# Seven-product units: the low part of unsummed weights by a negated copy and an adding transfer

## The chip, the cores and the metric

The kernel runs on one core of one Trainium2 chip. The metric is the device time of one execution in microseconds. Times of a run are medians over timed executions; a profile is one further execution with the hardware profiler on. Engine names in the profile: PE is TensorE (PEld its weight loads), DVE is VectorE, ACT is ScalarE, POOL is GpSimd, SP is SyncE, which issues the plain loads.

## What is computed

A two-layer transformer-like network with 256 latent and 256 context tokens of width 1024, in float32. Each layer is a half feed-forward, a mixer (attention in layer 0, an mLSTM in layer 1), and another half feed-forward, each modulated and normalized:

```python
def half_ffn(h, shift, scale, gate, w_in, w_out, g, b):
    xm = modulate(h, shift, scale)
    a, u = jnp.split(xm @ w_in, 2, axis=-1)
    y = (jax.nn.silu(a) * u) @ w_out
    return post_norm(h, 0.5 * gate * y, g, b)
```

`w_in` is 1024 x 5632 and `w_out` 2816 x 1024. There are four such feed-forwards; the first three run over all 512 tokens, the last over the 256 latent ones. The change touches the second half of `xm @ w_in` in the second and the third of them.

## The kernel before

Every float32 matrix product is made as three products in the faster type float32r: an operand `x` is split into a high part `h` (its rounded copy) and a low part `l = x - h`, and `mm3` adds `wh xh + wh xl + wl xh` in PSUM. A weight tile `[128, 1024]` is loaded by SP into one of three buffers of the tag `raw`. `split` then makes the parts: ScalarE casts (`h`, line 225 of before), VectorE subtracts (`l`, line 230). Both parts share one buffer of the tag `w`, of which there are 7.

The hidden columns of a feed-forward are 22 blocks `j` of 128 gate and 128 up columns, made in two halves of 11. In the second half of feed-forwards 2 and 3 (`fast` in `ffn`), `fast_in` makes a block by a scheme with seven products in place of eight: the weights are cut into `a11, a21` (buffer `r0`) and `a12, a22` (`r1`), the activations into latent and context tokens and lower and upper input rows. VectorE forms the weight sums `s1, s2, s4, s3` by four additions (line 641). Then four pairs are split: `a11` alone (512 wide), `r1`, which is `a12` and `a22` (1024 wide), `s1` with `s2`, and `s4` with `s3`. The seven products, in TensorE's order, are a11, a12, s1, s2, a22, s4, s3; each is 4 x 3 = 12 matmuls with 256 columns. ScalarE copies partial sums out after the first, third, fourth and fifth (lines 666, 669, 671, 673), applies silu (676) after the sixth, and VectorE finishes with 675, 679, 680 and the split of the result.

A scheduler in the tile framework orders each engine's instructions from its own costs; instructions that are pinned keep the program's order. Buffers of a tag are handed out as they come free. The norms use small buffers of the tag `s1` (`S1B` of them). [...]

Of the kernel before, what the change touches and what calls it, by code (L numbers as in the profile page):

```python
# [9 lines left out]
F32 = mybir.dt.float32  # L10
# [17 lines left out]
NFH = 11  # L28
# [5 lines left out]
SH = 16  # L34
# [24 lines left out]
HELD = 2  # L59
OUTAT = {18: (0,), 19: (1,), 21: (2,), 23: (3,), 25: (4,), 26: (5,)}  # L60
AHEAD = 3
S1B = 5

SQPE = ()
SQA = (7,)
# [21 lines left out]


SUMSAT = 4
FLIP = 56  # L90
BESIDE = {1: (), 2: (2, 3)}
PIECES = 4
# [50 lines left out]
class Stream:  # L143


    def __init__(self, b, chunks, sh=0):
        self.b, self.chunks, self.kept = b, chunks, (None, None)
        self.sh = sh if callable(sh) else lambda c: sh

    def __call__(self, i, w=P):  # L150
        c, o = divmod(i * P, 1024)
        if self.kept[0] != c:
            self.kept = (c, self.b.chunk(self.chunks[c], self.sh(c)))
        h, l = self.kept[1]
        return h[:, o : o + w], l[:, o : o + w]


class Keep(Stream):


    def __init__(self, b, chunks, sh=0, seen=None):
        super().__init__(b, chunks, sh)
        self.all = dict([seen.kept]) if seen else {}

    def __call__(self, i, w=P):
        c, o = divmod(i * P, 1024)
        if c not in self.all:
            self.all[c] = self.b.chunk(self.chunks[c], self.sh(c))
        h, l = self.all[c]
        return h[:, o : o + w], l[:, o : o + w]  # L170


class Body:
# [41 lines left out]
        w = self.t([P, 2 * 1024 + BLOCK], dt, tag="w", bufs=WB)  # L215
        return [w[:, i * 1024 + sh : i * 1024 + sh + n] for i in range(2)]

    def chunk(self, src, sh=0):
        r = self.raw(src)
        h, l = self.pair(sh=sh)  # L220
        self.split(r, h, l)
        return h, l

    def split(self, x, h, l):
        self.behind(self.nc.scalar.copy(h, x))  # L225
# [400 lines left out]
    def fast_in(self, j, w_in, st):  # L626

        nc, V, S = self.nc, self.nc.vector, self.nc.scalar
        half = 4 * P
        t4 = self.made[2]  # L630
        if j == NFH:
            w = self.t([P, 2 * 1024 + BLOCK], F32R, tag="w", bufs=WB)
            t4 = [w[:, FLIP + i * 1024 : FLIP + (i + 1) * 1024].rearrange("p (k f) -> p k f", f=TL) for i in range(2)]
            for i in range(2):
                S.copy(t4[i], self.made[2][i].bitcast(F32))
        r0, r1 = (self.raw(w_in[2 * j + i]) for i in range(2))
        sums = self.t([P, 4 * half], tag="sums", bufs=1, pool=st)
        part = lambda x, i: x[:, i * half : (i + 1) * half]
        a11, a21, a12, a22 = part(r0, 0), part(r0, 1), part(r1, 0), part(r1, 1)
        s1, s2, s4, s3 = (part(sums, i) for i in range(4))  # L640
        add = lambda o, x, y: V.tensor_tensor(out=o, in0=x, in1=y, op=ALU.add)  # L641
        ws = [self.pair(sh=SH, n=half)] + [self.pair(sh=SH) for _ in range(3)]
        self.split(a11, *ws[0])
        self.split(r1, *ws[1])
        add(s1, a21, a22)
        add(s2, s1, a11)
        add(s4, s2, a12)
        add(s3, a11, a21)
        self.split(sums[:, : 2 * half], *ws[2])
        self.split(sums[:, 2 * half :], *ws[3])  # L650
        w = {n: [part(x, i) for x in ws[p]] for n, p, i in (
            ("a11", 0, 0), ("a12", 1, 0), ("a22", 1, 1), ("s1", 2, 0), ("s2", 2, 1), ("s4", 3, 0), ("s3", 3, 1),
        )}
        of = lambda k0, g: lambda k: self.x(k0 + k, g)
        made = lambda i: lambda k: [x[:, k, :] for x in self.made[i]]

        def product(o, name, x, first, last):
            for k in range(ND // 2):
                c = slice(k * P, (k + 1) * P)
                self.mm3(o, [y[:, c] for y in w[name]], x(k), first and k == 0, last and k == ND // 2 - 1, group=False)  # L660

        x, yv, z = self.mm()[:, :TL], self.mm(), self.mm()[:, :TL]
        y, v = yv[:, :TL], yv[:, TL:]
        a, u = self.tmp(), self.tmp()
        product(x, "a11", of(0, LAT), True, False)
        S.copy(a[:, :TL], x)
        product(y, "a12", of(ND // 2, LAT), True, True)
        product(v, "s1", of(0, CTX), True, False)
        S.copy(u[:, TL:], v)
        product(x, "s2", made(0), False, False)  # L670
        S.copy(a[:, TL:], x)
        product(z, "a22", lambda k: [x[:, k, :] for x in t4], True, True)
        S.copy(u[:, :TL], z)
        product(v, "s4", of(ND // 2, CTX), False, True)
        V.tensor_tensor(out=a, in0=a, in1=yv, op=ALU.add)
        S.activation(a, a, AF.Silu)
        product(x, "s3", made(1), False, True)
        u2 = u.rearrange("p (n f) -> p n f", n=2)
        V.scalar_tensor_tensor(u2, x[:, None, :].broadcast_to([P, 2, TL]), -1.0, u2, ALU.mult, ALU.subtract)
        V.tensor_tensor(out=a, in0=a, in1=u, op=ALU.mult)  # L680
        gh, gl = self.gt[j] = tuple(self.t([P, self.gw], F32R, tag=k, bufs=self.gn, pool=self.gp) for k in ("gh", "gl"))
        self.split(a, gh, gl)

    def ffn(self, layer, s, gate, groups, side, start=None, cpool=None):
# [4 lines left out]
        with self.tc.tile_pool(name=f"ffn{li}", bufs=1) as gp:  # L689
# [34 lines left out]
            for hf in range(2):  # L724
                js = list(range(hf * NFH, (hf + 1) * NFH))[0 if hf else done :]
                if hf == 0 and not start:
                    first = js[:LEAD]
                    ws = {j: Keep(self, [w_in[2 * j + i] for i in range(2)], SH) for j in first}
                    assert len(self.running) == 1

                    k0, k1 = range(ND // 2), range(ND // 2, ND)
                    for j in first[:-1]:
                        unit_in(j, ws[j], LAT, LEADSTEP[li])
                    j = first[-1]
                    ps = unit_in(j, ws[j], LAT, ks=k0)
                    assert not self.running
                    xs = {}
                    for k in BESIDE[li]:
                        xs[k] = [self.t([P, self.gw], F32R, tag=t, bufs=self.gn, pool=gp)[:, FLIP : FLIP + TL] for t in ("gh", "gl")]
                        for o, x in zip(xs[k], self.x(k, CTX)):  # L740
                            nc.scalar.copy(o, x.bitcast(F32))
                    pc = unit_in(first[0], ws[first[0]], CTX, ks=k0, xs=xs)
                    ws[j](ND)
                    unit_in(first[0], ws[first[0]], CTX, ks=k1, ps=pc)
                    unit_in(j, ws[j], LAT, ks=k1, ps=ps)
                    for j in first[1:]:
                        unit_in(j, ws[j], CTX)
                    for j in first:
                        call("in", j)
                    js = js[LEAD:]  # L750
                fast = cpool is not None and hf == 1
                for j in js:
                    if fast:
                        self.fast_in(j, w_in, st)
                        continue
                    unit_in(j, stream(j), allg)
                    assert not self.running
                    if j >= LEAD + FAFTER:
                        self.fine = False
                    call("in", j)  # L760
                    self.residual(2, self.pin)
                if not hf:
                    self.residual(len(self.later))
                w = Stream(self, [w_out[hf * NFH + i] for i in range(NFH)])
                body = ND - TAIL if hf else ND
                if fast:
                    more.close()
                    cpool = self.silu_all()
                for d in range(body):
                    if cpool and not hf and d == SUMSAT:  # L770
                        self.flush()
                        cpool.close()
                        self.n += 1
                        more = ExitStack()
                        st = more.enter_context(self.tc.tile_pool(name=f"st{self.n}", bufs=1, side="right"))
                        self.fast_operands(st)
                    unit_out(hf, d, w, allg)
                    if cpool and not hf and d >= SUMSAT and d - SUMSAT < 2:
                        self.fast_sums(d - SUMSAT)
                    call("out", hf, d)  # L780
                if body < ND:
                    w = Keep(self, w.chunks, SH, w)
                    self.fine = True
                    for g in groups:
                        for d in range(body, ND):
                            unit_out(hf, d, w, g, TAILSTEP)
                    self.steps('B')
# [981 lines left out]
```

## Time and profile before

| | us |
|---|---|
| median of 3 runs | 1626.13 (1625.94 to 1628.58) |
| span of the profiled execution | 1625.5 |
| TensorE busy | 1606.9 (99%) |
| VectorE busy | 1355.7 (83%) |
| ScalarE busy | 749.2 (46%) |
| GpSimd busy | 63.0 (4%) |

The profiled execution is listed by its span, from the first to the last instruction; 1625.5 us is 0.6 us under the median of the timed runs. The first of the two stretches with seven-product units lies from about 742 to 847 us of the span, the second from about 1094 to 1199 us. A busy share is an average over stages; which engine ends a stage is read from the waits within it.

### The profile page before, as it was taken

The page shows a single profiled execution, that of the slowest core. Times are in us where ns is not written, and L with a number is a line of the kernel's source. Part 1 is how long each engine was busy: PE and PEld are TensorE (multiplying, and loading weights), DVE is VectorE, ACT ScalarE, POOL GpSimd, SP SyncE. Part 2 cuts the span into 40 slices and gives each one's busy share as a digit, 9 for nine tenths or more (in the row PEclk, how much of TensorE's full clock was granted, in tenths as well). Part 3 has the DMA queues.
Part 4 walks back from the last instruction along what each step waited for, and adds up shares of the span by engine and source line. Part 5 has one row for each costly group of instructions (what it writes and reads, how often), then busy time and mean ns, then how long its engine had stood idle before and what let it go on. Part 6 is the DMA issues. An engine that isn't in the chain of part 4 may idle for free. (4 is left out here: it accounts for less than half of the span.)

```text
span 1625.5 us, 26587 instructions
## 1 busy us (share of the span) xinstructions
PE 1606.9 (99%) x10304; PEld 1451.7 (89%) x10304; DVE 1355.7 (83%) x2699; ACT 749.2 (46%) x1272; POOL 63.0 (4%) x77
## 2 busy tenths in 40 slices
PE   9999999999999999999999999999999999999998
PEld 7888888889988998889998998889999989999987
DVE  7899977649889879899986879699966968897687
ACT  6522132314676443316652444336652657566542
POOL 0000000001011100000000100000001000030000
PEclk9999999999999999999999999999999999999999
DMA  9687766422202447633445258713363343437552
GB/s 358 221 252 237 235 205 187 137 66 85 66 1 80 151 134 221 219 117 105 129 146 180 79 165 289 253 58 118 104 225 100 98 130 87 142 110 253 181 176 91
DMA packets 72222, 251.56 MB, mean 155 GB/s; under 512 B 7960, under 2 KB 10776, under 8 KB 72096
## 3 DMA queue, kind: packets, MB, share of 16 engines
q1 hardware_dynamic: 71520, 249.09, 47.7%
q8 instruction: 80, 1.31, 0.3%
q10 hardware_dynamic: 576, 0.79, 0.1%
q14 instruction: 46, 0.38, 0.1%
HBM read 248.79 MB, written 1.05 MB: 154 GB/s over the span
## 5 line engine op out<-in xcount | busy, mean ns | idle before, releaser
L241 PE MATMUL t<-t,t 128*128 128x256 f32 (+2 forms) x8412 | 1317.0, 318 | 6.4 <-ACT t L225 3.3
L241 PEld LDWEIGHTS t<-t,t 128*128 128x128 f32 x8412 | 1185.7, 188 | 125.4 <-ACT t L225 4.7
L225 ACT CAST t<-t 128x1024 fp32r<-128x1024 f32 (+3 forms) x521 | 428.5, 844 | 485.8 <-PE t L241 214.5
L230 DVE TENSOR_TENSOR t<-t,t 128x256 fp32r<-128x256 f32 (+2 forms) x740 | 513.8, 729 | 111.9 <-ACT t L225 107.7
L350 DVE SCALAR_TENSOR_TENSOR t<-t,t 128x1024 bf16<-128x1024 f32 x224 | 260.7, 1220 | 0.0
L588 ACT ACTIVATE t<-t 128x512 f32<-128x512 f32 (+1 forms) x71 | 34.5, 490 | 103.5 <-PE t L241 102.4
L941 PE MATMUL t<-t,t 128*128 128x256 f32 (+1 forms) x256 | 79.3, 310 | 0.0
L718 DVE SCALAR_TENSOR_TENSOR t<-t,t,t 128x256 f32<-128x256 f32 x96 | 42.7, 478 | 43.9 <-PE t L241 43.7
L943 PE MATMUL t<-t,t 128*128 128x256 f32 (+1 forms) x256 | 78.4, 306 | 0.0
L942 PE MATMUL t<-t,t 128*128 128x256 f32 (+1 forms) x256 | 78.4, 306 | 0.0
L589 DVE TENSOR_TENSOR t<-t,t 128x512 f32<-128x512 f32 (+1 forms) x71 | 39.0, 553 | 40.6 <-PE t L241 28.1
L484 POOL TENSOR_TENSOR t<-t,t 128x256 f32<-128x256 f32 x30 | 23.4, 781 | 1104.9 <-ACT t L474 1103.5
L869 PE MATMUL t<-t,t 128*128 128x512 f32 (+1 forms) x300 | 60.5, 364 | 0.0
L869 PEld LDWEIGHTS t<-t,t 128*128 128x128 f32 x300 | 51.5, 189 | 8.9
L474 ACT ACTIVATE t<-t 128x256 f32<-128x256 f32 x72 | 26.1, 412 | 65.5 <-DVE t L467 65.5
L1456 PE MATMUL t<-t,t 128*128 128x512 f32 (+2 forms) x276 | 55.6, 356 | 0.0
L1456 PEld LDWEIGHTS t<-t,t 128*128 128x128 f32 (+1 forms) x276 | 44.9, 183 | 10.9 <-issue 0.9
L942 PEld LDWEIGHTS t<-t,t 128*128 128x128 f32 x256 | 48.1, 188 | 3.0 <-DVE t L230 0.5
L941 PEld LDWEIGHTS t<-t,t 128*128 128x128 f32 x256 | 48.3, 189 | 2.7
L943 PEld LDWEIGHTS t<-t,t 128*128 128x128 f32 x256 | 48.1, 188 | 2.5
L541 ACT ACTIVATE t<-t,t 128x256 fp32r<-128x256 f32 x72 | 32.8, 503 | 30.1 <-DVE t L540 30.1
L641 DVE TENSOR_TENSOR t<-t,t 128x512 f32<-128x512 f32 x66 | 45.2, 685 | 0.4
(206 smaller groups left out, 1078.6 us busy)
## 6 DMA issues: line engine op xcount, KB each, us to landing
t<-in_ffn_in SPq DMA_DIRECT2D x168, 512.0 KB, 4.1
t<-in_ada_w SPq DMA_DIRECT2D x138, 512.0 KB, 4.4
t<-in_ffn_out SPq DMA_DIRECT2D x66, 512.0 KB, 4.5
t<-in_ffn_last SPq DMA_DIRECT2D x22, 512.0 KB, 3.5
t<-in_att_in SPq DMA_DIRECT2D x12, 512.0 KB, 3.5
t<-in_att_out SPq DMA_DIRECT2D x8, 512.0 KB, 3.6
t<-in_ml_qk SPq DMA_DIRECT2D x8, 512.0 KB, 3.6
t<-in_ml_v SPq DMA_DIRECT2D x8, 512.0 KB, 3.5
```

The costliest lines, as they stand in the source:

```text
L225: self.behind(self.nc.scalar.copy(h, x))
L230: self.behind(self.nc.vector.tensor_tensor(out=ls, in0=xs, in1=hs.bitcast(F32), op=ALU.subtract))
L241: mm = lambda *k, **kw: self.nc.tensor.matmul(*k, skip_group_check=not group, **kw)
L350: ins = nc.vector.scalar_tensor_tensor(self.tmp().bitcast(BF16), r, 1.0, self.cb[:, v, :], ALU.mult, ALU.mult, accum_out=to)
L589: V.tensor_tensor(out=sl, in0=sl, in1=pu[:, :n], op=ALU.mult)
L641: add = lambda o, x, y: V.tensor_tensor(out=o, in0=x, in1=y, op=ALU.add)
L718: V.scalar_tensor_tensor(z, y[:, gg[0] - t0 : gg[1] - t0], gate()[:, v, d : d + 1], z, ALU.mult, ALU.add)
L869: pin(nc.tensor.matmul(o, gs[g], ws[k][w][:, i : i + n], start=k == k0 and g == w == 0, stop=k == k1 - 1 and g == 1,))
L941: mm(o, self.xh[:, k, c], wh, start=k == 0, stop=False)
L942: mm(o, self.xh[:, k, c], wl, start=False, stop=False)
L943: mm(o, self.xl[:, k, c], wh, start=False, stop=k == ND - 1)
L1456: mm = lambda *k, **kw: pin(nc.tensor.matmul(*k, **kw))
```

## The change

For the two pairs that need no sum, `a11` and `r1`, the low part is no longer made by VectorE. ScalarE writes the rounded copy `h` as before and then a second, negated copy of `h` into the place of the low part. A transfer issued by GpSimd then reads the same weights from HBM again and adds them to what lies there, so that the place holds `x - h`. The sums' pairs and all other splits stay as they are. To make room, the norms' small buffers go from 5 to 4, and the descriptor buffer from 512 to 1024 bytes. The flag for the same in the output weights (`ADDOUT`) is off, so the new arguments of `Stream`, `Keep` and `chunk` change nothing.

```diff
-S1B = 5
+S1B = 4
...
+ADDIN = True
+ADDOUT = False
...
+    def added(self, x, h, l, src):
+
+        S = self.nc.scalar
+        S.copy(h, x)
+        S.activation(l, h.bitcast(F32), AF.Copy, scale=-1.0)
+        self.nc.gpsimd.dma_start(l, src.bitcast(F32R), accum_op=ALU.add)
...
         ws = [self.pair(sh=SH, n=half)] + [self.pair(sh=SH) for _ in range(3)]
-        self.split(a11, *ws[0])
-        self.split(r1, *ws[1])
+        if ADDIN:
+            self.added(a11, *ws[0], w_in[2 * j, :, :half])
+            self.added(r1, *ws[1], w_in[2 * j + 1])
+        else:
+            self.split(a11, *ws[0])
+            self.split(r1, *ws[1])
...
-    nc = _bacc.Bacc("TRN2", target_bir_lowering=False, num_devices=1, dynamic_dma_scratch_size=512)
+    nc = _bacc.Bacc("TRN2", target_bir_lowering=False, num_devices=1, dynamic_dma_scratch_size=1024)
```

Lines of the changed kernel differ in number: its copy `h` of the two pairs is line 230, the negation 231, the transfer 232; 225 became 235, 230 became 240, 666 to 673 became 680 to 687.

The order changes on ScalarE, VectorE, GpSimd and, by three matmuls, on TensorE. ScalarE at the start of the first stretch, before. The names: t1213 is the pair of `a11` of the first unit, t1214 that of its `r1`, t1215 and t1216 those of the sums, t1227 and t1228 the `a11` and `r1` of the second unit, and t1209 a copy of activations.

```order
L635 CAST t1209_7146<-t1185_6935 128x1024
L225 CAST t1213_7154<-t1210_7149 128x512
L635 CAST t1209_7146<-t1185_6935 128x1024
L225 CAST t1214_7155<-t1211_7151 128x1024
L225 CAST t1215_7156<-t1212_7153 128x1024
L225 CAST t1216_7157<-t1212_7153 128x1024
L225 CAST t1227_7276<-t1224_7271 128x512
L225 CAST t1228_7277<-t1225_7273 128x1024
L666 COPY t1220_7173<-t1217_7170 128x256
```

The same place after:

```order
L645 CAST t1209_7146<-t1185_6935 128x1024
L230 CAST t1213_7154<-t1210_7149 128x512
L645 CAST t1209_7146<-t1185_6935 128x1024
L231 ACTIVATE t1213_7154<-t1213_7154 128x512
L230 CAST t1214_7155<-t1211_7151 128x1024
L235 CAST t1215_7156<-t1212_7153 128x1024
L231 ACTIVATE t1214_7155<-t1214_7155 128x1024
L235 CAST t1216_7157<-t1212_7153 128x1024
L230 CAST t1227_7278<-t1224_7273 128x512
L231 ACTIVATE t1227_7278<-t1227_7278 128x512
L230 CAST t1228_7279<-t1225_7275 128x1024
L231 ACTIVATE t1228_7279<-t1228_7279 128x1024
```

The negation of t1214 stands behind the cast of t1215, and four negations stand ahead of the copy after the first product.

TensorE at the second product of the first unit (a12, into t1218), before, with what an instruction waits for:

```order
L241 MATMUL t1217_7170<-t3_67,t1213_7154 128x256
L241 MATMUL t1218_7171<-t3_67,t1214_7155 128x256 [waits Activation_49]
L241 MATMUL t1218_7171<-t4_68,t1214_7155 128x256
L241 MATMUL t1218_7171<-t3_67,t1214_7155 128x256 [waits DVE_49]
L241 MATMUL t1218_7171<-t3_67,t1214_7155 128x256
```

And after:

```order
L251 MATMUL t1217_7172<-t3_67,t1213_7154 128x256
L251 MATMUL t1218_7173<-t3_67,t1214_7155 128x256 [waits DVE_49,Activation_49]
L251 MATMUL t1218_7173<-t4_68,t1214_7155 128x256
L251 MATMUL t1219_7174<-t1209_7146,t1214_7155 128x256 [waits DVE_49,PE_49]
L251 MATMUL t1219_7174<-t1209_7146,t1214_7155 128x256
L251 MATMUL t1231_7296<-t3_67,t1227_7278 128x256 [waits DVE_49,Activation_49]
L251 MATMUL t1218_7173<-t3_67,t1214_7155 128x256 [waits DMASW1_49]
L251 MATMUL t1218_7173<-t3_67,t1214_7155 128x256
```

The first matmul with a low part waits for GpSimd's transfer (DMASW) where it waited for VectorE. Three matmuls of later products (two of a22 into t1219, one of the next unit into t1231) were moved ahead of that wait. In the second stretch TensorE's order is the same as before.

ScalarE in the steady part, before (t1290 is the unit in work, t1311 and t1312 are the `a11` and `r1` of two units later):

```order
L671 COPY t1290_7783<-t1287_7780 128x256
L225 CAST t1311_8008<-t1308_8003 128x512
L673 COPY t1291_7784<-t1289_7782 128x256
L225 CAST t1312_8009<-t1309_8005 128x1024
L225 CAST t1313_8010<-t1310_8007 128x1024
L676 ACTIVATE t1290_7783<-t1290_7783 128x512
```

And after:

```order
L685 COPY t1290_7795<-t1287_7792 128x256
L230 CAST t1311_8022<-t1308_8017 128x512
L231 ACTIVATE t1311_8022<-t1311_8022 128x512
L687 COPY t1291_7796<-t1289_7794 128x256
L230 CAST t1312_8023<-t1309_8019 128x1024
L231 ACTIVATE t1312_8023<-t1312_8023 128x1024
L690 ACTIVATE t1290_7795<-t1290_7795 128x512
```

Each cast of the two pairs is followed by its negation, and the cast of the first sums' pair (t1313) moved behind the silu. GpSimd's queue has in each stretch 22 transfers in turn, 512 and 1024 wide, between the sums of one norm and those of the next.

More of the change, by code (lines that the diff above doesn't have):

```diff
@@ L143, with __init__ @@
 class Stream:
-    def __init__(self, b, chunks, sh=0):
+    def __init__(self, b, chunks, sh=0, add=False):
         self.b, self.chunks, self.kept = b, chunks, (None, None)
+        self.add = add
         self.sh = sh if callable(sh) else lambda c: sh
@@ L152, in __call__ @@
         if self.kept[0] != c:
-            self.kept = (c, self.b.chunk(self.chunks[c], self.sh(c)))
+            self.kept = (c, self.b.chunk(self.chunks[c], self.sh(c), self.add))
         h, l = self.kept[1]
@@ L158, with __init__ @@
 class Keep(Stream):
-    def __init__(self, b, chunks, sh=0, seen=None):
-        super().__init__(b, chunks, sh)
+    def __init__(self, b, chunks, sh=0, seen=None, add=False):
+        super().__init__(b, chunks, sh, add)
         self.all = dict([seen.kept]) if seen else {}
@@ L167, in __call__ @@
         if c not in self.all:
-            self.all[c] = self.b.chunk(self.chunks[c], self.sh(c))
+            self.all[c] = self.b.chunk(self.chunks[c], self.sh(c), self.add)
         h, l = self.all[c]
@@ L216, in pair, with chunk @@
         return [w[:, i * 1024 + sh : i * 1024 + sh + n] for i in range(2)]
-    def chunk(self, src, sh=0):
+    def chunk(self, src, sh=0, add=False):
         r = self.raw(src)
         h, l = self.pair(sh=sh)
-        self.split(r, h, l)
+        (self.added if add else self.split)(r, h, l, *((src,) if add else ()))
         return h, l
+    def added(self, x, h, l, src):
[3 more added lines that the diff above has]
+        self.nc.gpsimd.dma_start(l, src.bitcast(F32R), accum_op=ALU.add)
     def split(self, x, h, l):
@@ L763, in ffn @@
                     self.residual(len(self.later))
-                w = Stream(self, [w_out[hf * NFH + i] for i in range(NFH)])
+                w = Stream(self, [w_out[hf * NFH + i] for i in range(NFH)], add=ADDOUT)
                 body = ND - TAIL if hf else ND
@@ L781, in ffn @@
                 if body < ND:
-                    w = Keep(self, w.chunks, SH, w)
+                    w = Keep(self, w.chunks, SH, w, w.add)
                     self.fine = True
```

## The prediction

> **What bounds the kernel now.** I read the page's head first, then TensorE's time line around the code that changes, then the busy time of every engine there, and last ScalarE's order of time at the two places where that code begins.
>
> ```profile
> span 1625.5 us, 26587 instructions
> PE 1606.9 (99%) x10304; PEld 1451.7 (89%) x10304; DVE 1355.7 (83%) x2699; ACT 749.2 (46%) x1272; POOL 63.0 (4%) x77
> ```
>
> TensorE is busy for 99% of the span. The mean can hide a stage in which it waits, so the next view is TensorE's time line, merged while nothing interrupts it (start, length, line, count, idle time ahead in brackets).
>
> ```profile
> 699.76 190.35 PE L241 MATMUL t<-t,t 128*128 128x512 f32 x1352
> 1059.83 182.19 PE L241 MATMUL t<-t,t 128*128 128x512 f32 x1316
> ```
>
> The change touches only the 22 seven-product units, 11 in each of two stretches. The first stretch lies between 742 and 847 us, the second between 1094 and 1199 us. Both lie inside these unbroken pieces: no wait of TensorE stands in either, nor in the 43 us behind each. The busy times of exactly those stretches (us busy, instructions in brackets, granted clock, share of the DMA engines, GB/s):
>
> ```profile
> 742.00:847.00 105.00, 105.00 (x925) 104.96 (x924) 97.20 (x128) 67.17 (x109) 0.00 (x0) 1.00 0.39 123
> 1094.00:1199.00 105.00, 105.00 (x925) 104.96 (x925) 95.52 (x127) 67.12 (x110) 0.00 (x0) 1.00 0.40 122
> ```
>
> A unit is 7 products of 12 matmuls, 84 in all; 925 matmuls in 105 us are 0.1135 us each, so a product takes 1.36 us and a unit 9.53 us. VectorE is loaded to 93% (97.20 of 105), yet TensorE does not wait for it. That is the main reading: the engine which the change relieves is nearly full, but it is not the one that ends anything, and the clock is full. What is taken off VectorE is worth nothing here, unless it shortens TensorE's own work, which it does not.
>
> **The change part by part.** The groups of instructions in the first stretch (busy us, mean ns), and one group of the whole kernel for an ACTIVATE of the new size, with the POOL group that is nearest to what POOL gets:
>
> ```profile
> L230 DVE TENSOR_TENSOR t<-t,t 128x1024 fp32r<-128x1024 f32 x36 | 44.0, 1222 | 7.6 <-ACT t L225 5.3 <-PE t L241 1.9
> L225 ACT CAST t<-t 128x1024 fp32r<-128x1024 f32 x36 | 37.9, 1052 | 16.4 <-PE t L241 13.0 <-DVE t L641 2.8 <-DMA t<-in_ffn_in 0.3
> L230 DVE TENSOR_TENSOR t<-t,t 128x512 fp32r<-128x512 f32 x20 | 13.7, 684 | 0.0
> L225 ACT CAST t<-t 128x512 fp32r<-128x512 f32 x19 | 11.8, 622 | 2.9 <-DVE t L680 2.7
> L673 ACT COPY t<-t 128x256 f32<-128x256 f32 x11 | 4.1, 374 | 3.4 <-PE t L241 3.3
> L862 ACT ACTIVATE t<-t,t 128x1024 fp32r<-128x1024 f32 x22 | 25.1, 1152 | 27.4 <-DVE t L860 25.3 <-PE t L241 2.1
> L484 POOL TENSOR_TENSOR t<-t,t 128x256 f32<-128x256 f32 x30 | 23.4, 781 | 1104.9 <-ACT t L474 1103.5
> ```
>
> Removed: one 512-wide and one 1024-wide subtraction per unit on VectorE, 0.68 + 1.22 = 1.9 us. VectorE falls from 97.2 / 11 = 8.8 us a unit to 6.9. Worth on the path: 0, as shown.
>
> Added on ScalarE: the two negated copies, 0.62 + 1.15 = 1.8 us a unit (the 512-wide one at the CAST's 622 ns, the 1024-wide one at L862's 1152 ns). ScalarE rises from 67.2 / 11 = 6.1 to 7.9 us of 9.53. It still fits; 1.6 us a unit remain as cover.
>
> Added on POOL and the DMA queues: 44 transfers, 256 and 512 KB, which read the weights a second time and add them to what lies in the buffer. POOL does nothing else in these stretches (0.00 in both rows), and what stands behind them on its queue are the next norm's sums, over 40 us later. 11 x 768 KB in 105 us are 82 GB/s beside 123. At the present share per GB/s that is 0.26 more, 0.52 if an added byte counts twice: 0.65 to 0.91 of the DMA engines. Not full, but transfers will take longer than now.
>
> The low part of these weights now arrives later after its high part: negation, issue, landing, where a subtraction was. Call X the time from the end of the negation until TensorE may read. The trace has no transfer that POOL issues and none that adds, so X is bounded by the plain ones (KB, median us from issue to landing):
>
> ```profile
> t<-in_ffn_last SPq DMA_DIRECT2D x22, 512.0 KB, 3.5
> t<-in_first SPq DMA_DIRECT2D x1, 17.0 KB, 1.8
> t<-in_start_in SPq DMA_DIRECT2D x1, 512.0 KB, 9.1
> ```
>
> Lower end 3.5 us, upper end 9.1 (issued among many others). Between them: 1.8 us hardly depend on size, 1.7 us are the movement of 512 KB. An add must read two operands, so I take twice the movement, 1.8 + 3.4 = 5.2, and 0.8 for POOL to issue it (the 781 ns that it takes for a pass over 128 rows): X = 6.0 us. It lies nearer to the 3.5 than to the 9.1 because the DMA share here is 0.4. For 256 KB the same gives 0.8 + 1.8 + 1.7 = 4.3.
>
> [...]
>
> Inside a stretch X is hidden. ScalarE works two units ahead: after the copy L673, which follows the fifth product of unit u, it makes the copy and the negation of unit u + 2, 0.37 + 1.05 + 1.15 = 2.6 us. The second product of unit u + 2 needs the low part 10 products later, 13.6 us. So X may be 11.0 us before the steady units wait.
>
> At the start of a stretch there is no such lead. ScalarE's order of time there, first and second stretch:
>
> ```profile
> 736.06 1.05 ACT L635 CAST t<-t 128x1024 fp32r<-128x1024 f32 x1
> 737.01 3.46 ACT L225 CAST t<-t 128x1024 fp32r<-128x1024 f32 x4
> 742.34 1.05 ACT L225 CAST t<-t 128x1024 fp32r<-128x1024 f32 x1 [1.88 <-PE t L241]
> 743.76 0.38 ACT L666 COPY t<-t 128x256 f32<-128x256 f32 x1 [0.36 <-PE t L241]
> ...
> 1086.64 3.46 ACT L225 CAST t<-t 128x1024 fp32r<-128x1024 f32 x4
> 1094.26 1.05 ACT L225 CAST t<-t 128x1024 fp32r<-128x1024 f32 x1 [4.16 <-PE t L241]
> 1095.67 0.37 ACT L666 COPY t<-t 128x256 f32<-128x256 f32 x1 [0.36 <-PE t L241]
> ```
>
> The 742.34 row is released by the last matmul of the stage before, and L666 by the end of the first product: the first product runs from 742.15 and the second from about 743.6, where its third matmul needs the low part at 743.8. In the new order ScalarE does, from 737.0, the 512-wide negation, the r1 copy, one sum's copy, then the r1 negation: 0.62 + 1.05 + 1.05 + 1.15, less 0.1 of overlap at each of three joins, ends at 740.6. Lead 3.2 us. Three later matmuls now stand ahead of that wait, 0.34 us. So TensorE stands X - 3.2 - 0.34 = 2.5 us. Second stretch: the negation ends at 1086.64 + 3.6 = 1090.2, needed at 1095.7, lead 5.5; it stands 0.5 us. The 512-wide one, ready at 737.6 and 1087.3, is needed at 742.4 and 1094.3: leads 4.8 and 7.0 against 4.3, no wait.
>
> What else is late at the start: ScalarE's next units move back by 2.4 us (0.62 + 1.15 + 0.62), into its idle 1.88 and 4.16 us; the copy L666 then ends near 745.4, and the fourth product, which overwrites what L666 reads, starts at 746.3 or later. No second wait.
>
> S1B from 5 to 4 and the descriptor buffer: no instruction is added, and outside the two stretches the order of the engines and what they wait for is the same. Tiles move by 512 bytes; no row shows that an address costs time. Taken as 0, with 0 to 1 us kept open.
>
> Sum: 2.5 + 0.5 = 3.0 us, and nothing later takes it back, since TensorE is the bound behind both places. The profiled span is 1625.5, and the median of the three timed runs is 1626.13; the work around the span does not change, so 1626.1 + 3.0 = 1629.1 us. 0.2% of it, about what a measurement here can tell from no change, is 3.3 us.
>
> **The rivals.**
>
> *Hidden transfer (not slower).* If X stays under 4.6 us, the first stretch stands under 1.1 us and the second not at all: 1626.1 to 1627.2. For it: plain 512 KB loads land in 3.5. Against it: the second operand and the issue by POOL. It decides at the first start alone, at X = 3.5.
>
> *The clock halves.* This has happened once in the kernel (same columns as above, then TensorE's waits in those 10 us: total, times, longest):
>
> ```profile
> 450.00:455.00 5.00, 4.33 (x32) 3.78 (x30) 3.64 (x12) 3.51 (x8) 0.00 (x0) 1.00 0.01 2
> 455.00:460.00 5.00, 3.84 (x18) 3.46 (x19) 4.84 (x15) 2.83 (x10) 1.01 (x1) 0.66 0.00 0
> PE t L241 <- DVE t L230: 1.2, 1, 1.2
> PE t L241 <- ACT t L225: 0.7, 1, 0.7
> ```
>
> TensorE stood for 0.67 + 1.16 = 1.8 us of these 10, and the clock was 0.66 in the second 5: 0.34 x 5 = 1.7 us lost. A stand of 2.5 us could bring the same: 1629.1 + 1.7 = 1630.8. [...]
>
> *The transfers are slow.* At X = 9.1 the starts cost 5.6 + 3.6 = 9.2, 12.6 with the clock twice: 1635 to 1639. Beyond X = 11 every unit waits; two units then take 2.6 + X plus four products (5.4 us), so at X = 13 a unit is 10.5 us instead of 9.53, 1.0 x 9 x 2 = 18 us more beside starts of 17: 1661. For it: DMA share up to 0.91, and nothing in the trace prices an add. Against it: X would have to be over three times a plain load.
>
> *Faster.* It would need a wait of TensorE that goes, and there is none for 190 and 182 us.
>
> **How the numbers follow.** The forecast (X from 4.6 to 7.2, no clock drop) 0.48, with 0.18 of it over 1629.4; hidden 0.20, of which 0.03 is drift below -0.2%; clock drop 0.17; slow transfers 0.15. Slower by over 0.2%: 0.18 + 0.17 + 0.15 = 0.50; faster 0.03; within 0.47. The range is from X = 3.5 (1626.2) to X near 9 without a second clock drop (1637); it leaves out X above that, 0.09, and 0.05 below.
>
> **What would show it.** Right: TensorE's time line breaks near 744 us, at the second product of the first unit, waiting for a DMA that POOL issued, for about 2.5 us; a break of under 1 us near 1096; no other break up to the norm; issues by POOL with 512 KB near 5 to 6 us to landing; VectorE 21 us less busy in each stretch, ScalarE about 19 us more. Wrong: no break at all (X under 3.5), breaks in every unit (X over 11), or a clock below 1.00 in the 10 us behind the first break.

## The result and the profile after

| | before | after |
|---|---|---|
| median, us | 1626.76 (4 runs, 1625.94 to 1628.58) | 1637.28 (4 runs, 1634.92 to 1640.22) |
| ratio | | 1.0059, 95% interval 1.0041 to 1.0077 |
| span of the profiled execution, us | 1625.5 | 1637.5 |

The change costs 10.5 us, 0.6%. That is the direction forecast, but over three times the 3.0 us of the sum, and at the top of the range: the time lies 0.3 us above its 1637, the change just inside the 10.9 that 1637 is over 1626.1. That the range reaches so far is luck: its upper part was drawn for transfers with X near 9, and X did not bring most of the loss.

The head of the page and the busy times of the two stretches, moved along with the code (columns as before: us, busy by engine with instructions, clock, DMA share, GB/s):

```profile
span 1637.5 us, 26710 instructions
PE 1612.4 (98%) x10304; PEld 1455.7 (89%) x10304; DVE 1323.3 (81%) x2655; ACT 781.7 (48%) x1316; POOL 101.0 (6%) x121
...
742.00:847.00 105.00, 102.58 (x897) 101.86 (x896) 81.70 (x107) 79.27 (x128) 17.48 (x21) 1.00 0.85 200
1098.00:1203.00 105.00, 102.78 (x881) 102.30 (x881) 78.24 (x103) 77.99 (x124) 16.59 (x19) 0.98 0.82 190
```

VectorE is relieved as the change intends, 97.2 to 81.7 us in the first stretch, and it buys nothing. ScalarE is 12 us busier (67.2 to 79.3), and the DMA share doubles (0.39 to 0.85). TensorE, busy for all 105 us before, now lacks 2.4 and 2.2 us in the two stretches. Its time line shows where:

```profile
744.27 2.00 PE L251 MATMUL t<-t,t 128*128 128x256 f32 x15 [1.36 <-DMA t<-in_ffn_in]
746.79 19.05 PE L251 MATMUL t<-t,t 128*128 128x256 f32 x165 [0.52 <-DMA t<-in_ffn_in]
766.38 127.19 PE L251 MATMUL t<-t,t 128*128 128x256 f32 x983 [0.54 <-DMA t<-in_ffn_in]
893.43 0.70 PE L457 MATMUL t<-t,t 128*128 128x256 f32 x2
...
1100.47 22.51 PE L251 MATMUL t<-t,t 128*128 128x256 f32 x190 [0.39 <-DMA t<-in_ffn_in]
1124.80 126.31 PE L251 MATMUL t<-t,t 128*128 128x256 f32 x961 [1.83 <-ACT t L680]
1250.97 0.70 PE L457 MATMUL t<-t,t 128*128 128x256 f32 x2
```

In the first stretch the waits are for transfers: the first unit's a11 (744) and r1 (746), and the third unit's r1 (766). In the second there is a small one of the forecast kind (1100), and a larger one that was not forecast: 1.83 us for ScalarE's copy L680. The first matmuls of the next norm, before, to set against the rows 893.43 and 1250.97:

```profile
889.97 0.70 PE L447 MATMUL t<-t,t 128*128 128x256 f32 x2
1241.88 0.70 PE L447 MATMUL t<-t,t 128*128 128x256 f32 x2
```

At the first of these norms the kernel is 3.46 us late (0.37 of it from ahead of the stretch, by the starts of the same matmuls in both traces), at the second 9.09, and the span is 12.0 longer. Behind the wait of 1.83 the clock fell:

```profile
1126.00:1130.00 4.00, 4.00 (x24) 4.00 (x23) 3.93 (x6) 2.65 (x7) 0.88 (x1) 0.58 0.80 179
```

0.42 x 4 = 1.7 us lost: the clock was 0.50 for 3.4 us from 1125.98. What kept ScalarE from its copy is in its order of time:

```profile
1115.99 0.35 ACT L687 COPY t<-t 128x256 f32<-128x256 f32 x1
1119.62 1.05 ACT L230 CAST t<-t 128x1024 fp32r<-128x1024 f32 x1 [3.27 <-DMA t<-in_ffn_in]
1120.70 1.06 ACT L231 ACTIVATE t<-t 128x1024 fp32r<-128x1024 f32 x1
1122.92 0.63 ACT L690 ACTIVATE t<-t 128x512 f32<-128x512 f32 x1 [1.15 <-DVE t L689]
1123.45 1.03 ACT L235 CAST t<-t 128x1024 fp32r<-128x1024 f32 x1
1124.39 0.36 ACT L680 COPY t<-t 128x256 f32<-128x256 f32 x1
```

ScalarE took these in program order. It stood 3.27 us for a raw load of the fourth unit, and the third unit's copy L680, which TensorE needed, was queued behind the cast and negation of that load. The DMA issues of the first stretch, after (KB, median us from issue to landing; the q0 row is GpSimd's queue with its packets, MB and share of the engines), and SP's row before:

```profile
q0 software_dynamic: 3164, 8.64, 47.8%
t<-in_ffn_in SPq DMA_DIRECT2D x17, 512.0 KB, 5.4
t<-in_ffn_in POOLq DMA_DIRECT2D x11, 512.0 KB, 7.7
t<-in_ffn_in POOLq DMA_DIRECT2D x10, 256.0 KB, 7.2
```

```profile
t<-in_ffn_in SPq DMA_DIRECT2D x17, 512.0 KB, 3.7
```

An adding transfer lands 7.2 (256 KB) or 7.7 us (512 KB) after its issue here, and the raw loads beside it take 5.4 us where they took 3.7. The load that ScalarE stood for, the fourth unit's `r1`, was issued at 1110.42 and landed at 1119.54, 9.1 us later: the third unit's two adding transfers (issued at 1108.83 and 1109.78, the larger landing at 1119.33) and a raw load of the fifth unit (1111.59) were under way with it. With the 3.7 us of before it would have landed at 1114.1, 2.2 us ahead of the end of ScalarE's copy L687, and ScalarE would not have stood for it.

### The profile page after: what moved, and what is told of

It reads as the page before. It is cut to its first block, busy times and chain, and to the rows that moved or that the text cites. A ratio compares the mean times of both kernels' runs of the same rounds, so it can differ in the third digit from the quotient of the medians.

```text
span 1637.5 us, 26710 instructions
## 1 busy us (share of the span) xinstructions
PE 1612.4 (98%) x10304; PEld 1455.7 (89%) x10304; DVE 1323.3 (81%) x2655; ACT 781.7 (48%) x1316; POOL 101.0 (6%) x121
## 5 line engine op out<-in xcount | busy, mean ns | idle before, releaser
L235 ACT CAST t<-t 128x1024 fp32r<-128x1024 f32 (+3 forms) x477 | 391.2, 844 | 451.1 <-PE t L251 191.4
L240 DVE TENSOR_TENSOR t<-t,t 128x256 fp32r<-128x256 f32 (+2 forms) x696 | 472.1, 715 | 120.5 <-ACT t L235 112.3
L232 POOL DMA_DIRECT2D t<-in_ffn_in x44 | 38.6, 876 | 487.5 <-ACT t L231 216.7
```

The lines of the kernel that those rows point to most:

```text
L240: self.behind(self.nc.vector.tensor_tensor(out=ls, in0=xs, in1=hs.bitcast(F32), op=ALU.subtract))
```

## The experiments

The median of before was 1628.1 to 1628.7 us in these runs, so kernels are compared by ratio; 0.001 is 1.6 us. "Breaks" are waits of TensorE inside the two stretches.

**The room alone.** Edit:

```diff
-ADDIN = True
+ADDIN = False
```

> The two splits are back, S1B = 4 and the descriptor buffer of 1024 bytes stay. Theory (all of the loss of 10.5 us comes from the adding transfers): the time of before, 1625 to 1629 us, no wait of TensorE from 742 to 847 and from 1094 to 1199. Rival (the room and the tiles that move cost time): 1629 us or more, with more matmuls at the slower pitch of 118 ns.

Measured: 1628.32 us, ratio 1.0003 (0.9994 to 1.0011), no break. The smaller `S1B` and the larger descriptor buffer (the size that `dynamic_dma_scratch_size` sets) cost nothing that can be measured.

**ScalarE's work without the transfers.** Edit, in `added`:

```diff
-        self.nc.gpsimd.dma_start(l, src.bitcast(F32R), accum_op=ALU.add)
+        self.nc.vector.tensor_tensor(out=l, in0=x, in1=l.bitcast(F32), op=ALU.add)
```

> Copy and negated copy stay on ScalarE, but VectorE adds the raw weights to the negated copy; there is no transfer. ScalarE has all its added work (about 19 us per stretch), VectorE its old load. Theory (the landing time of the transfers and their load on the DMA engines): no wait of TensorE over 0.6 us in the stretches, 1625 to 1630 us. Rival (ScalarE's 1.7 us more per unit make it late): 1632 us or more, waits of TensorE on L680.

Measured: 1629.19 us, ratio 1.0008 (1.0000 to 1.0017), no break. ScalarE's added work is hidden, as the prediction had it (in the second execution below, but for 0.28 us). Yet the profiled span was 1629.8, 4.3 us over that of before. Most of this shows in how many matmuls fit into the same 75 us of the first stretch: before, this kernel, and this kernel executed once more (the twelfth run):

```profile
770.00:845.00 75.00, 75.00 (x665) 75.00 (x664) 69.02 (x91) 48.05 (x80) 0.00 (x0) 1.00 0.40 125
```

```profile
770.00:845.00 75.00, 75.00 (x639) 75.00 (x639) 69.68 (x92) 57.13 (x90) 0.00 (x0) 1.00 0.39 117
```

```profile
770.00:845.00 75.00, 74.72 (x659) 74.52 (x658) 69.80 (x92) 57.95 (x92) 0.00 (x0) 1.00 0.40 124
```

The clock is 1.00 and TensorE is busy, but for the 0.28 us of the third row, yet a matmul with 256 columns takes 75 / 665 = 113 ns in one execution and 75 / 639 = 117 ns in another. This time from one start to the next is called the pitch below. In the first trace of this kernel the step from 113 to 118 ns comes at 768.5 us, where no wait of TensorE is listed, and stays for 695 matmuls (about 3.1 us).

> The kernel of the second run once more, for one look at the pitch of the 256-column matmuls, which was 118 ns instead of 113 from 768.5 to 850 us of the first look, though TensorE waited for nothing. If the pitch is fixed by the program, the same 695 matmuls are slow again; if it is drawn anew in each execution, the piece at 118 ns has another place or length, and the span differs by up to 3 us from 1629.8.

Measured, one execution: span 1627.7, with 113 ns in both stretches (659 matmuls in the third row above, and 532 in the 60 us from 1135, as in before) but for their starts, which are slower in before, too (118 ns over the first 60 matmuls from 742); the one break, of 0.28 us for L680 at 785, left the pitch as it was. So in these two executions the pitch was not fixed by the program.

**The same transfers without the addition.** The low part is then the raw weight. Edit:

```diff
-        self.nc.gpsimd.dma_start(l, src.bitcast(F32R), accum_op=ALU.add)
+        self.nc.gpsimd.dma_start(l, src.bitcast(F32R))
```

> The transfers stay in place and size, but they overwrite instead of adding (the low part is then the raw weight, so the output is another). Theory (an adding byte takes about twice the time of a plain one on the DMA engines): 512 KB land in 4 to 5 us after issue instead of 7.6, DMA share in the stretches 0.6 instead of 0.85, raw loads back to about 4 us; TensorE waits 1 to 2 us at the first start, none at the second; 1627 to 1631 us. Rival (any second read of the weights costs this much): landing stays at 7 us and the time at 1634 us or more.

Measured: 1630.79 us, ratio 1.0013 (1.0004 to 1.0021). Its one break, and the DMA rows of its first stretch:

```profile
741.16 29.01 PE L251 MATMUL t<-t,t 128*128 128x256 f32 x243 [0.37 <-DMA t<-in_ffn_in]
```

```profile
q0 software_dynamic: 2922, 7.97, 24.5%
t<-in_ffn_in SPq DMA_DIRECT2D x17, 512.0 KB, 4.5
t<-in_ffn_in POOLq DMA_DIRECT2D x10, 512.0 KB, 4.9
```

7.97 MB in 24.5% of 105 us are 310 GB/s; the adding ones moved 8.64 MB in 47.8%, 172 GB/s. An adding byte kept the engines 1.8 times as long. TensorE waits less than the 1 to 2 us expected, and in this execution the first stretch, too, ran at 118 ns (639 matmuls in the 75 us from 770). The second read alone costs little, 0.13%; the addition makes the difference.

**Which units.** In `fast_in` the added form holds only for some of the eleven units of a stretch (`NFH` is 11, and `j` of the first unit is 11):

```diff
-        if ADDIN:
+        if ADDIN and j >= NFH + 3:
```

That is from the fourth unit on. The conditions of the next four runs are, in their order, `j < NFH + 3`, `j >= NFH + 1`, `j != NFH + 2` and `j >= NFH + 2`.

> The first three units of each stretch by the old split, the other eight by the adding transfers. Theory (the loss is at the starts, where ScalarE and the transfers have no lead): no wait of TensorE at either start, none later, clock 1.00: 1626 to 1630 us. Rival (the transfers cost time in every unit, by contention): 8/11 of the loss stays, 1633 to 1636 us.

Measured: 1629.33 us, ratio 1.0008 (1.0000 to 1.0017), and no break. Its first stretch and the rows of its transfers there:

```profile
742.00:847.00 105.00, 105.00 (x920) 104.77 (x919) 85.64 (x112) 78.75 (x125) 14.06 (x16) 1.00 0.77 185
...
t<-in_ffn_in POOLq DMA_DIRECT2D x8, 512.0 KB, 7.9
```

Landing is as late as in the full change and the DMA share 0.77, yet TensorE is busy for all 105 us. Eight units of eleven cost at most 0.0017.

> The mirror of the fourth run: only the first three units of each stretch use the adding transfers, the other eight the old split. Theory (the whole loss is made at the two starts): TensorE's time line breaks as after the change (1 to 3 us near 744, up to 4 us with the lower clock between 1100 and 1126), 1633 to 1639 us, though only 12 of the 44 transfers are left. Rival (the loss is spread over the units): 3/11 of it, about 1630 us.

Measured: 1640.52 us, ratio 1.0073 (1.0060 to 1.0085), at least as much as the whole change, with 12 of the 44 transfers. TensorE's breaks (first stretch, second):

```profile
742.92 2.00 PE L251 MATMUL t<-t,t 128*128 128x256 f32 x15 [1.61 <-DMA t<-in_ffn_in]
745.91 24.28 PE L251 MATMUL t<-t,t 128*128 128x256 f32 x201 [0.98 <-DMA t<-in_ffn_in]
...
1126.77 3.44 PE L251 MATMUL t<-t,t 128*128 128x256 f32 x18 [2.10 <-ACT t L680]
```

With the run before, this puts the loss in the first three units of each stretch. It is not all waiting: in this execution the first stretch also ran at 118 ns behind its breaks (639 matmuls in the 75 us from 770, where before has 665), which is 2.9 us in those 75.

> Only the first unit of each stretch by the old split, ten units by the adding transfers. Theory: the first unit's own landings go (1.9 us at 744 and 746, 0.4 at 1100); the waits of the second and third unit (0.5 us near 766, 1.8 us on L680 near 1125, with the lower clock behind it) come from loads of raw weights that share the engines with adding transfers, and ScalarE has a unit more of lead then, so they shrink: 1627 to 1632 us. Rival (the wait on L680 doesn't depend on the first unit): it stays, with the clock: 1632 to 1635 us.

Measured: 1635.71 us, ratio 1.0043 (1.0030 to 1.0055). The rival holds: the waits for landings are gone, the wait on L680 stands in both stretches, and the clock fell behind the second, to 0.59 in the 4 us from 1123.

```profile
767.89 2.33 PE L251 MATMUL t<-t,t 128*128 128x256 f32 x18 [1.95 <-ACT t L680]
...
1122.28 5.98 PE L251 MATMUL t<-t,t 128*128 128x256 f32 x36 [2.18 <-ACT t L680]
```

> Only the third unit of each stretch by the old split, all other units by the adding transfers. Theory (the wait on L680 is made by the third unit's two transfers, issued within 1 us of each other and of the fourth unit's two raw loads, so that a raw load takes 9 us and ScalarE's cast of it stands in front of the second unit's copies): the first unit's waits stay (about 2 us near 744, 0.4 near 1100), the wait on L680 and the lower clock go: 1629 to 1633 us. Rival (any unit's transfers do the same, the wait only moves on): a wait on L680 of 1.5 us or more, 1634 us or more.

Measured: 1637.64 us, ratio 1.0057 (1.0044 to 1.0070). The waits are those of the theory: landings in the first stretch, 0.4 us in the second, none on L680, and the clock at 1.00.

```profile
743.06 2.01 PE L251 MATMUL t<-t,t 128*128 128x256 f32 x15 [1.49 <-DMA t<-in_ffn_in]
745.56 24.67 PE L251 MATMUL t<-t,t 128*128 128x256 f32 x207 [0.49 <-DMA t<-in_ffn_in]
```

The time is not: 1629 to 1633 was expected. In the profiled execution (1636.1 us) the second stretch ran at 118 ns:

```profile
1135.00:1195.00 60.00, 60.00 (x512) 60.00 (x511) 44.16 (x57) 45.34 (x73) 10.48 (x12) 1.00 0.83 185
```

Before has 532 matmuls in such 60 us. If the whole stretch ran so, 105 x (1 - 512/532) = 3.9 us, an estimate, were lost by it, more than by all its waits (2.4 us). That the other four executions lost their time in the same way is not shown.

> The first two units of each stretch by the old split, nine by the adding transfers. Theory: the third unit's transfers still fill the DMA engines together with the raw loads, but ScalarE, without the first two units' negations (1.7 us each), is up to 3 us further ahead, about the 3.1 to 3.3 us that its cast waited: a wait on L680 below 1 us, 1627 to 1631 us. Rival (the third unit alone decides): the wait of 1.9 to 2.2 us with the lower clock stays in both stretches, 1634 to 1637 us.

Measured: 1636.54 us, ratio 1.0049 (1.0036 to 1.0063). The rival again, with the smaller wait in the first stretch, which in this execution ran at 118 ns behind it (640 matmuls in the 75 us from 770):

```profile
767.02 3.21 PE L251 MATMUL t<-t,t 128*128 128x256 f32 x25 [1.34 <-ACT t L680]
...
1125.55 2.79 PE L251 MATMUL t<-t,t 128*128 128x256 f32 x14 [2.27 <-ACT t L680]
```

Taken together: without the third unit's two transfers (all but third, from fourth) there is no wait on L680 over 0.2 us; with both there is, except in the first stretch of the full change and of the first three, where the waits for landings come before it. Two units without negations did not give ScalarE lead enough (waits of 1.34 and 2.27 us).

**Which transfer.** Edits: in `if ADDIN`, one of the two lines becomes `self.split(a11, *ws[0])` or `self.split(r1, *ws[1])`.

> Only the 512 KB transfers (r1); a11 by the old split. Theory: at the first start the second product waits 1 to 2 us for its transfer, the first product not at all; the load on the DMA engines falls by a third (share 0.7), raw loads take 4 to 5 us and no wait on L680 comes: 1628 to 1632 us. Rival (the number of bytes is not what slows the raw loads): as after the change, 1634 us or more.

Measured: 1639.62 us, ratio 1.0072 (1.0058 to 1.0086), the time of the rival, but not by its way. Its main breaks:

```profile
745.98 23.47 PE L251 MATMUL t<-t,t 128*128 128x256 f32 x190 [2.08 <-DMA t<-in_ffn_in]
...
1102.22 3.00 PE L251 MATMUL t<-t,t 128*128 128x256 f32 x24 [1.77 <-DMA t<-in_ffn_in]
```

There is half a microsecond on L680 in the first stretch; behind the 2.08 the clock fell (0.98 in the mean of that stretch's 105 us), and behind the 1.77 TensorE ran at 118 ns (512 matmuls in the 60 us from 1135, where before has 532). Why the transfer behind the 1.77 took 7.6 us from its issue, where that of the full change took 5.7, is not settled.

> Only the 256 KB transfers (a11); r1 by the old split. Theory: the first product waits about 1 to 1.4 us near 744 (its lead is about 4 us, the transfer takes 5 to 6 with its issue), nothing else; DMA share 0.55; 1627 to 1631 us. Rival (the small transfer is hidden and the loss all comes from the 512 KB ones): no wait at all, 1626 to 1628 us.

Measured: 1631.22 us, ratio 1.0020 (1.0010 to 1.0029), and no break in either stretch, so the waits of the theory did not come: the first transfer landed 4.2 us after its issue, where that of the full change took 5.9. The raw load behind it was issued 1.9 us later here, 0.6 us later there. The 3 us are in none of the stretches' waits; the profile shows 1.7 us by 1500 us of the span, in small pieces, and 1.8 in the last feed-forward, which the change does not touch. Their cause stays open.

**The descriptor buffer.** Edit:

```diff
-dynamic_dma_scratch_size=1024
+dynamic_dma_scratch_size=512
```

> The changed kernel with the descriptor buffer of 512 bytes instead of 1024. Theory (the buffer's size is no part of the loss): the time of the changed kernel, 1634 to 1640 us, issues of 870 ns and landings of 7 to 8 us. Rival (512 bytes hold fewer descriptors, POOL waits to issue): issues longer than 870 ns and 1641 us or more.

Measured: 1674.27 us, ratio 1.0288 (1.0270 to 1.0305). I was wrong: the buffer matters, though not by longer issues (median 875 ns against 870). GpSimd's transfers at the start of the first stretch, and their landing over the whole kernel:

```profile
743.97 0.89 POOL L232 DMA_DIRECT2D t<-in_ffn_in  x1 [5.17 <-DVE t L651]
749.58 0.87 POOL L232 DMA_DIRECT2D t<-in_ffn_in  x1 [4.71 <-issue]
755.36 0.89 POOL L232 DMA_DIRECT2D t<-in_ffn_in  x1 [4.91 <-PE t L251]
...
t<-in_ffn_in POOLq DMA_DIRECT2D x22, 512.0 KB, 5.6
t<-in_ffn_in POOLq DMA_DIRECT2D x22, 256.0 KB, 4.2
```

Where the first four issues of the full change are 2.1 to 2.8 us apart, with up to three transfers under way, here 5.3 to 6.2 us lie between the first six. Each lands sooner (5.6 and 4.2 us against 7.6 and 7.2 in the full change), but it starts later, and TensorE stands 17.2 us in the first stretch alone. The releasers named in the rows are not what these issues needed: the negations that they add to had ended at 740.30, 742.42 and 744.44. That an issue waited until the transfer ahead had landed is my reading of these times; what the buffer holds, and why 512 bytes allow no more, is not shown.

No variant beat the kernel before, which has no wait in these stretches to remove.

## Why the prediction was right or wrong, point by point

- *TensorE is the bound, relief of VectorE is worth 0.* Right: the from-fourth run relieves VectorE (97.2 to 85.6 us) and gains nothing (ratio 1.0008).
- *ScalarE's extra work fits.* Right: the vector-add run (ratio 1.0008, no wait of TensorE over 0.28 us).
- *DMA share 0.65 to 0.91.* Right: 0.85 and 0.82; an added byte counts 1.8 times, the forecast allowed 2.
- *X = 6.0 us for 512 KB, 4.3 for 256 KB.* The first was right at the start of the first stretch: the negation ended 0.3 us before the issue at 741.18 and the transfer landed at 746.75, X = 5.9. The second was mis-sized: the first a11 transfer took 5.9 us from its issue, X = 6.2 instead of 4.3, with a raw load issued 0.6 us behind it. The longer time goes with that load, not with r1's transfer: with the load and without r1's transfer beside it (512-byte buffer) it took 5.9 us as well, with the load 1.9 us behind it (a11 alone) 4.2. That an add reads two operands no run shows; measured are the 1.8 times of a byte, and 0.87 us for the issue against the 0.8 taken. So the first product waited 1.36 us, where none was forecast, and the second only 0.52 instead of 2.5. The total of the first start, 1.9, is near the forecast because r1's landing sets it; the wait for a11 only brought part of it forward.
- *Steady units are hidden up to X = 11.* Right as far as it was tried: X is about 8 in the steady units (0.3 + 7.7), and no unit from the fourth on makes TensorE wait.
- *Second start, 0.5 us.* Right: 0.39.
- *VectorE 21 us less busy, ScalarE 19 more in each stretch.* Mis-sized: 15.5 and 12.1 in the first. The durations of single instructions were added up; in busy time the overlap of neighbours counts once (the four casts at 737.01 of before: 3.46 us, where their durations add up to 3.8), and the 105 us hold fewer matmuls than before (897 against 925).
- *"No second wait" (the copy L666, now L680).* This is the step that failed. The prediction looked at ScalarE's own work and at the landing of the new transfers, and named the slower loads without following who waits for them. The third unit's transfers slowed the fourth unit's raw load to 9.1 us, ScalarE stood 3.3 us for it in order, and TensorE stood 1.83 us for L680. With the third unit on the old split this wait is gone, though the time is not (1637.64 us, with a slow pitch in its trace).
- *The rival "clock halves".* It came true, on top of the forecast: 1.7 us at 1126, where the rival had 1.7 us from the row at 455. It came behind the wait that the sum did not have; behind the two at 744 and 746 the clock stayed full (1.00 in the stretch). 1.83 us of stand came ahead of it, and the clock was 0.50 for 3.413 us.
- *`S1B` and the buffer 0.* Right for the room as a whole. But the larger buffer is no mere room: without it the change cost 46 us (1674.3 against 1628.7), a rival that the prediction did not have.

The sum of the profiled execution: waits of TensorE in the stretches 4.6 us (2.4 and 2.2) against 3.0 forecast; the clock 1.7; together 6.3 of the 12.0. Of the rest, 1.8 us are longer pitches that the starts of the same matmuls in both traces show: 0.7 at 940 to 960 (in the trace of the room alone, too), 0.9 at 1464 to 1490, 0.2 net in the two stretches. About 1 us is the restart of TensorE at the five breaks, some 0.2 us each beyond the wait: from the first matmul behind one to the next it is 221 to 229 ns instead of 113. Some 3 us are not traced to a cause: 0.4 lie ahead of the first stretch, 0.4 between 1440 and 1450 us (in the trace of the room alone, too), 0.3 near 1610, 1.1 behind the start of the last matmul, the rest in small pieces. Single executions of before alone differ by 5 us.

## What to carry to other kernels

Where TensorE has no wait, taking work from a nearly full engine is worth nothing (VectorE 97.2 to 85.6 us, ratio 1.0008), and a new break can cost more than its length: here the clock was 0.50 for 3.4 us behind one of 1.83 us, and five of fourteen stretches with a break ran at 118 ns instead of 113. When traffic is added, follow every load that shares the DMA engines with it (the raw loads took 5.4 us instead of 3.7) to the engine that waits for it, and what stands behind that wait in program order; look first at the starts of stages, where nobody has a lead. If a transfer is to be hidden, begin with it a few units into the stage: from the fourth unit on, the same transfers cost at most 0.17%.

## What the runs showed of the hardware that was not expected

- An adding transfer issued by GpSimd moved 172 GB/s in the time it occupied the DMA engines (full change, first stretch), a plain one on the same queue 310 (no addition). From issue to landing, in the median: 5.6 us for 512 KB with the 512-byte buffer, 7.7 in the full change, where they overlap each other and the raw loads; 0.87 of it the issue.
- With a descriptor buffer of 512 bytes GpSimd's first eight issues lay 4.7 to 8.6 us apart; with 1024 bytes the first four lay 2.1 to 2.8 apart, and up to three transfers (512, 256 and 512 KB) were under way at once.
- A run of matmuls with 256 columns had a pitch of 113 or of 118 ns and could change between them where no wait is listed (vector add, 768.5 us); which it took differed between two executions of one program. It is worth up to about 4 us in a stretch here, and TensorE counts as busy all the while. Leaving aside the starts of the stretches and the run with the 512-byte buffer, five of the fourteen stretches with a break of TensorE ran at 118 ns (639 or 640 matmuls in the 75 us from 770, or 512 in the 60 us from 1135, where before has 665 and 532), and of the twelve without a break one (vector add, 639). Why a break sometimes brings it is open.
- The clock fell behind stands of 1.83 us (full change), 2.08 (r1 alone), 2.10 (first three), 2.18 (from second) and 2.27 (from third): it is 0.98 in the mean of those stretches' 105 us. It is 1.00 in the stretches whose longest stand was 1.34, 1.36, 1.49, 1.61, 1.77 or 1.95 us (the 512-byte buffer is left out). So the length of a stand alone does not decide. In the traces of before and of the full change the drops between 100 and 1600 us, at 456.49, and at 456.96 and 1125.98, lasted 3.413 us each at 0.50; the last two start 669.01 us apart, to 0.1 us 196 times that length. Cut into steps of that length, counted from a drop, these two traces show TensorE standing for 1.83 us or more in the step just ahead of each drop, and for 1.77 or less in every other step between 100 and 1600. What decided at the stand of 1.95 (from second), which brought none, is open.
